# A two-layer hybrid attention block on one core: weights stored so that a partition's part of each load is one contiguous run

## The chip, the cores and the metric

The kernel runs on one core of one Trainium2 chip. The metric is the device time of one execution in microseconds (us), as the median of several runs; lower is better.

## The reference

Two layers of a diffusion trunk work on 512 latent tokens and 256 context tokens, 1024 wide, in float32. In each layer

```python
sh, sc, gt = split(silu(c) @ w_ada[l] + b_ada[l], 3)           # w_ada: 1024 x 3072, also for c_ctx
h  = rms_norm(x, norm_g[l]) * (1 + sc) + sh                    # latent and context rows
qa, ka, va, ga, qb, kb, vb, gb, qn, kn, vn, gn = split(h @ w_in[l])   # w_in: 1024 x 3584
ya = rms_norm(diff_attend(qa, ka, va)) * silu(ga)              # group A
yb = gqa_attend(qb, kb, vb) * silu(gb)                         # group B
yn = neighbourhood_attend(qn, kn, vn, rpb) * silu(gn)          # group C
x  = x + gt * (concat(ya, yb, yn) @ w_out[l])                  # w_out: 1024 x 1024
```

Latent queries attend to latent and context keys; context queries, in the first layer only, to context keys. Queries and keys are normalised, and those of A and B rotated. Only the latent rows of the second layer are returned.

## The kernel before

All activations are held transposed, 128 features on the partitions in KT = 8 blocks, 768 tokens on the free axis (512 latent, 256 context). The three large weights are the only big reads: 25 MB of `w_ada`, 29 MB of `w_in` and 8 MB of `w_out` for both layers, counted from their shapes.

**Modulation.** `w_ada` is read in blocks of 128 output columns, each as two DMAs of 256 KB (4 blocks of 128 input rows by 128 columns). For the first layer's shift and scale, 16 blocks are loaded in eight pairs by `ada_load` (issued at L185) into buffers that later hold probabilities (`hl`, `pt`) or spare ones (`adw`, `stg`), and `ada_pair` (matmuls at L198) turns each pair into a column of the scale and shift. `build_h` (L426 and after) needs that column for the block `kt` of normalised activations. The other 32 blocks come from the generator `ada_blocks` (L214), which is stepped now and then while projections run: its load (L221) goes into two `adw` buffers, one block ahead, its matmuls are at L236, and VectorE copies and adds at L241 to L250.

**Projections.** `w_in`'s columns are cut into ten chunks of 384 or 256 columns, listed in the dictionary `CH` by column ranges; chunk a1 is put together from two ranges (128 and 256 columns). Each chunk is loaded in four pieces of 256 input rows (two blocks of 128 partitions). `w_out` is loaded in four column blocks of 256 columns, in pieces of 2 or 3 input blocks (`OKT`). All these pieces go through one stream, `WStream`: `_load` (DMA at L69) into three `raw` buffers, then `_split`, which makes of each float32 weight a rounded part `whi` on ScalarE (L82) and a remainder `wlo` on VectorE or GpSimd (L85), with room for HLB = 6 split pieces. A piece that also needs the norm of value columns gets squares on ScalarE (L278). `done` frees a split piece and lets the stream advance. The projection matmuls (`mm3`, L685 to L687) multiply hi by hi, hi by lo and lo by hi; the output's are at L1093 to L1095.

**Attention.** For each unit of queries: scores on TensorE into two score tiles (L781), row maxima on VectorE (L836), exponentials on ScalarE (L850), a cast to float16 (L870) with a remainder on VectorE or GpSimd (L871), a transposing DMA `pt<-hl` (L873), and the product with the values (L906, L907). While a group's attention runs, `both` (L1060) mixes in the next chunks' projections.

**Order.** Every DMA is issued by SyncE (SP) in one order, and each engine works through its own list in order. The lists are fixed at build time: the program is written in Python in the order described, with priorities shifted for some steps (`prio`), and the tile framework then orders the instructions with a planner that runs a simulated timeline (L1355, `schedule_with_timeline_sim=True`). Its estimates of durations, those of DMAs included, can move instructions relative to each other.

The work begins with 3 MB of activations (L1205), then the eight pairs of modulation blocks, between them the first four pieces of `w_in` (chunk a0), whose projection `proj_first` interleaves with `ada_pair` and `build_h`.

Of the kernel before, what the change touches and what calls it, by code (L numbers as in the profile page):

```python
# [24 lines left out]
DEPTH = 2  # L25
D = 1024
KT = 8
# [5 lines left out]
BT = 6 * 256 + 6 * 192 + 256  # L33


REST = {"C": 7}
AK = [[6, 2, 0, 2], [0, 1, 0, 2]]
VSHARE = {"HA": (0, 1), "H": (0, 1), "G": (1, 1), "T": (1, 4), "HC": (1, 8), "WB": (1, 2), "WC": (1, 1),
# [71 lines left out]
def tile_hybrid_block(ctx: ExitStack, tc: tile.TileContext, xT_d, cT_d, ng_d, w_ada, bT_d, w_in, w_out,  # L110
# [7 lines left out]
    V, A, G, PE, SP = nc.vector, nc.scalar, nc.gpsimd, nc.tensor, nc.sync  # L118
# [56 lines left out]
    def ada_load(l, bs, spare=False):  # L175

        ts = []
        for b in bs:
            for r in range(2):
                if spare:  # L180
                    t = sb([128, 576], F32, "stg", 2) if r else sb([128, 512], F32, "adw", 2)
                else:
                    t = sb([128, 768], F32, *(("pt", 4) if r else ("hl", 4)))
                t = t[:, 0:512].rearrange("p (k n) -> p k n", n=128)
                SP.dma_start(out=t, in_=w_ada[l, 512 * r:512 * r + 512, 128 * b:128 * b + 128].rearrange(  # L185
                    "(k p) n -> p k n", p=128))
                ts.append(t)
        return l, bs, ts

# [24 lines left out]
    def ada_blocks(blocks):  # L214


        def load(l, b):
            ts = []
            for r in range(2):
                t = sb([128, 512], F32, "adw", 2).rearrange("p (k n) -> p k n", n=128)  # L220
                SP.dma_start(out=t, in_=w_ada[l, 512 * r:512 * r + 512, 128 * b:128 * b + 128].rearrange(  # L221
                    "(k p) n -> p k n", p=128))
                ts.append(t)
            return ts

        nxt = load(*blocks[0])
        yield
        for i, (l, b) in enumerate(blocks):
            if l not in mods:
                new_mods(l)  # L230
            ts = nxt
            ps = (psV if share.phase == "1" else psP).tile([128, 512], F32, tag="pv" if share.phase == "1" else "p",
                                                           name="ada")
            for r in range(2):
                for g in range(4):
                    PE.matmul(ps[32 * g:32 * g + 32, 0:128], lhsT=cS[:, 4 * r + g, :], rhs=ts[r][:, g, :],  # L236
                              start=(r == 0), stop=(r == 1), tile_position=(0, 32 * g))
            if i + 1 < len(blocks):
                nxt = prio(-100)(load)(*blocks[i + 1])
            t = sb([128, 128], F32, "adt", 1)  # L240
            V.tensor_copy(t, ps[:, 0:128])  # L241
            src = ps[:, 128:130]
            PE.matmul(src, lhsT=t, rhs=sel, start=True, stop=True)
            w, kt = divmod(b, 8)
            if w == 1:
                V.tensor_scalar(out=mods[l][0][:, kt, :], in0=src, scalar1=bT1[:, l, kt:kt + 1],
                                scalar2=ng[:, l, kt:kt + 1], op0=ALU.add, op1=ALU.mult)
            else:
                V.tensor_scalar(out=mods[l][1 if w == 0 else 2][:, kt, :], in0=src, scalar1=bT[:, l, b:b + 1],
                                scalar2=None, op0=ALU.add)  # L250
            yield

    def ada_step():
# [1 line left out]
        next(st["ada"], None)  # L255


    CH = {
# [4 lines left out]
    }  # L263
    FA = ["b0", "b1", "gb"]
    FB = ["c0", "c1", "c2", "gn"]
    FC = ["y", "o"]
# [1 line left out]
    F1 = ["a1", "ga"]  # L268
    ORDER = [c for c in ["a0"] + F1 + FA + FB + FC if c in CH]
    VCOL = {"a0": (256, 384), "a1": (0, 128), "b0": (128, 256), "c1": (0, 384)}  # L270
    vn = {}

    def v_norm(l, c, q):
        def emit(raw, lo):
            a, b = VCOL[c]
            if q == 0:
                vn[l, c] = sb([128, 8], F32, "vn" + c, 1)
            A.activation(out=lo[:, :, a:b], in_=raw[:, :, a:b], func=AF.Square,  # L278
                         accum_out=vn[l, c][:, q:q + 1])
        return emit  # L280

    OKT = {"ab": [(0, 3), (3, 2)], "n": [(5, 3)]}
    pieces, pidx = [], {}
    for l in range(DEPTH):
        for c in ORDER:
            cols, n = CH[c]
            pidx[l, c] = []
            for q in range(4):
                srcs, off = [], 0
                for c0, w in cols:  # L290
                    srcs.append((w_in[l, 256 * q:256 * q + 256, c0:c0 + w].rearrange("(k p) n -> p k n", p=128),
                                 off, w))
                    off += w
                pidx[l, c].append(len(pieces))
                pieces.append(("w", n, 2, srcs) + ((v_norm(l, c, q),) if c in VCOL else ()))
        for part in ("ab", "n"):
            for oc in range(4):
                pidx[l, part, oc] = []
                for k0, nk in OKT[part]:
                    src = w_out[l, 128 * k0:128 * k0 + 128 * nk, 256 * oc:256 * oc + 256].rearrange(  # L300
                        "(k p) n -> p k n", p=128)
                    pidx[l, part, oc].append(len(pieces))
                    pieces.append(("w", 256, nk, [(src, 0, 256)]))
    W = WStream(nc, pool, pieces, share)
# [348 lines left out]
    def ctx_cols(l, c):  # L653
        n = CH[c][1]
        if l == 0:
# [33 lines left out]
    def proj_first(l, c, groups, before):  # L689

        open_group(l, c[0].upper())
        n = CH[c][1]
        for gi, js in enumerate(groups):
# [366 lines left out]
    def both(l, g, chunks, lead=0):  # L1060
# [13 lines left out]
        for x, _ in enumerate(attn(l, g)):  # L1074
            want = min(nf, lead + (nf - lead - REST.get(g, 0)) * (x + 1) // (na - (YE if g == "B" else 0)))
            while done[0] < want:
# [213 lines left out]
def _layout(x, c, ctx, c_ctx, norm_g, w_ada, b_ada, w_in, w_out, diff_q_norm, diff_k_norm, lambda_q1, lambda_k1,  # L1290
            lambda_q2, lambda_k2, diff_subln, gqa_q_norm, gqa_k_norm, nat_q_norm, nat_k_norm, nat_rpb):
    import numpy as np

    ca = np.ascontiguousarray
    lat = np.asarray(x)[0].reshape(8, 64, D).transpose(1, 0, 2).reshape(NL, D)
    both = np.concatenate([lat, np.asarray(ctx)[0]], 0)
    d = {}
    d["xT"] = ca(both.T.reshape(KT, 128, NT).transpose(1, 0, 2))
    cc = np.stack([np.asarray(c)[0], np.asarray(c_ctx)], 1)
    d["cT"] = ca(cc.reshape(KT, 128, 2).transpose(1, 0, 2))  # L1300
    d["ng"] = ca(np.asarray(norm_g).reshape(DEPTH, KT, 128).transpose(2, 0, 1))
    d["w_ada"] = ca(np.asarray(w_ada))
    d["bT"] = ca(np.asarray(b_ada).reshape(DEPTH, 24, 128).transpose(2, 0, 1))
    d["w_in"] = ca(np.asarray(w_in))
    d["w_out"] = ca(np.asarray(w_out))
    d["small"] = ca(np.concatenate([np.asarray(a) for a in (
        diff_q_norm, diff_k_norm, gqa_q_norm, gqa_k_norm, nat_q_norm, nat_k_norm,
        lambda_q1, lambda_k1, lambda_q2, lambda_k2, diff_subln)], 1))
    f = np.float32
    t = np.arange(NL)  # L1310
    row, col = (t % 8).astype(f), (t // 8).astype(f)
    parts = []
    for dim in (32, 64):
        nf = dim // 4
        inv = np.power(f(10000.0), -np.arange(nf, dtype=f) / f(nf)).astype(f)
        ang = np.concatenate([row[:, None] * inv, col[:, None] * inv], 1).astype(f)
        parts += [np.cos(ang).astype(f), np.sin(ang).astype(f)]
    d["rope"] = ca(np.concatenate(parts, 1).reshape(4, 128, 96).transpose(1, 0, 2))
    rpb = np.asarray(nat_rpb)
    p = np.arange(128)  # L1320
    qi, qr = p // 8, p % 8
    k = np.arange(256)
    kw, kr = k // 8, k % 8
    tab = np.full((DEPTH, 128, BT), 0.0, f)
    ok = (kw[None] >= qi[:, None]) & (kw[None] < qi[:, None] + 16)
    dr = kr[None] - qr[:, None] + 7
    dc = np.clip(kw[None] - qi[:, None] + 7, 0, 30)
    qc = np.where(qi < 8, 56 + qi, qi - 8)
    kc = np.where((qi < 8)[:, None], 48 + kw[None, :128], kw[None, :128])
    dc3 = kc - qc[:, None] + 15  # L1330
    for h in range(6):
        g = rpb[:, h][:, dr, dc]
        g[:, ~ok] = -1e18
        tab[:, :, 256 * h:256 * h + 256] = g
        tab[:, :, 1536 + 192 * h:1536 + 192 * h + 128] = rpb[:, h][:, dr[:, :128], dc3]
    d["btab"] = tab
    return d
# [24 lines left out]
```

## Time and profile before

| | |
|---|---|
| three runs | 935.75, 937.06, 941.35 us; median 937.06 |
| profiled execution, device time | 930.04 us |
| its span in the trace | 928.2 us |
| mean granted TensorE clock | 0.95 |
| read from HBM, written to HBM | 86.55 MB, 15.47 MB |
| DMA packets | 361,449 |
| of these under 512 B | 256,656 |
| 512 B to under 2 KB | 98,560 |
| 2 KB to under 8 KB | 5,888 |

In the profile, PE is TensorE's matrix multiply and PEld its weight load, DVE is VectorE, ACT ScalarE, POOL GpSimd, SPq the queue of SyncE, which issues DMAs. A group of instructions is named by its line and as `out<-in` by tile names, so `raw<-in_w_in_dram` is a load of a projection piece and `pt<-hl` a transposing DMA. In a row of waits stand the engine and line that waited, the work that ended the wait, then the total in us, the number of times and the longest. In a row of one line or tile, three numbers with slashes are the shortest, median and longest duration in ns (in us where the row says so). The slices are fortieths of the span, a digit being tenths. In a row `q1 hardware_dynamic` stand packets, MB and the time that the packets took as a share of 16 DMA engines over the span or the stretch asked for; it can pass 100% where packets of one engine overlap.

### The profile page before, as it was taken

The page shows a single profiled execution, that of the slowest core. Times are in us where ns is not written, and L with a number is a line of the kernel's source. Part 1 is how long each engine was busy: PE and PEld are TensorE (multiplying, and loading weights), DVE is VectorE, ACT ScalarE, POOL GpSimd, SP SyncE. Part 2 cuts the span into 40 slices and gives each one's busy share as a digit, 9 for nine tenths or more (in the row PEclk, how much of TensorE's full clock was granted, in tenths as well). Part 3 has the DMA queues.
Part 4 walks back from the last instruction along what each step waited for, and adds up shares of the span by engine and source line. Part 5 has one row for each costly group of instructions (what it writes and reads, how often), then busy time and mean ns, then how long its engine had stood idle before and what let it go on. Part 6 is the DMA issues. An engine that isn't in the chain of part 4 may idle for free.

```text
span 928.2 us, 17966 instructions
## 1 busy us (share of the span) xinstructions
PE 829.5 (89%) x6386; PEld 709.7 (76%) x6386; DVE 682.7 (74%) x1306; ACT 592.3 (64%) x1269; POOL 541.3 (58%) x502
## 2 busy tenths in 40 slices
PE   5899997997998999797999989989959999988978
PEld 3788886786887889685777889878849888866757
DVE  5975788988678866467765797789877975855853
ACT  5334577885887687476563445478758978757740
POOL 2638846998798465432441047939988776732420
PEclk9899999998999999899999999999979999987979
DMA  9925895644979997989898713884556889995642
GB/s 307 331 90 135 204 215 133 154 85 127 194 156 221 195 221 170 227 213 229 183 234 235 243 61 101 184 189 101 140 132 156 168 188 249 240 253 134 134 114 83
DMA packets 361449, 165.47 MB, mean 178 GB/s; under 512 B 256656, under 2 KB 355216, under 8 KB 361104
## 3 DMA queue, kind: packets, MB, share of 16 engines
q1 hardware_dynamic: 361360, 164.33, 73.9%
q8 instruction: 50, 0.82, 0.4%
q14 instruction: 39, 0.32, 0.1%
HBM read 86.55 MB, written 15.47 MB: 110 GB/s over the span
## 4 chain that ended last, share of the span: by engine, by line
PE 46%; DVE 15%; DMA 13%; POOL 9%; issue 8%; ACT 7%; SPq 1%; DVEq 0%; POOLq 0%; ACTq 0%
PE proj L685 7%; PE proj L687 7%; PE proj L686 6%; PE sc L781 5%; DMA pt<-hl 4%; PE pv L906 3%; PE op L1093 3%; PE op L1094 3%; PE op L1095 2%; ACT p L850 2%; DVE mx L836 2%; DMA raw<-in_w_in_dram 2%; DMA stB<-in_btab_dram 2%; POOL hl L871 2%; POOL wlo L85 1%
## 5 line engine op out<-in xcount | busy, mean ns | idle before, releaser
L871 POOL TENSOR_TENSOR hl<-p,hl 128x768 f16<-128x768 f32 (+3 forms) x138 | 204.2, 1484 | 179.7 <-ACT hl L870 139.7
L685 PE MATMUL proj<-whi,bigL 128*128 128x384 f32 (+1 forms) x592 | 203.4, 344 | 9.8 <-DVE tb L608 3.8
L686 PE MATMUL proj<-wlo,bigL 128*128 128x384 f32 (+1 forms) x592 | 200.3, 338 | 0.9 <-POOL wlo L85 0.7
L687 PE MATMUL proj<-whi,bigL 128*128 128x384 f32 (+1 forms) x592 | 197.7, 336 | 0.0
L850 ACT ACTIVATE p<-sc,nb,gsc 128x768 f32<-128x768 f32 (+3 forms) x200 | 166.0, 844 | 14.3 <-DVE p L866 5.0
L836 DVE TENSOR_REDUCE mx<-sc 128x1 f32<-128x768 f32 (+2 forms) x128 | 118.7, 931 | 31.7 <-PE sc L781 31.2
L685 PEld LDWEIGHTS proj<-whi,bigL 128*128 128x128 f32 x592 | 115.4, 195 | 19.9 <-DVE tb L608 5.4
L870 ACT CAST hl<-p 128x768 f16<-128x768 f32 (+3 forms) x144 | 103.7, 725 | 33.0 <-DMA pt<-hl 18.5
L686 PEld LDWEIGHTS proj<-wlo,bigL 128*128 128x128 f32 x592 | 115.5, 195 | 3.9 <-POOL wlo L85 1.6
L687 PEld LDWEIGHTS proj<-whi,bigL 128*128 128x128 f32 x592 | 114.4, 194 | 3.3 <-issue 2.4
L85 POOL TENSOR_TENSOR wlo<-raw,whi 128x768 fp32r<-128x768 f32 (+1 forms) x44 | 82.9, 1893 | 30.0 <-ACT whi L82 24.8
L82 ACT CAST whi<-raw 128x768 fp32r<-128x768 f32 (+1 forms) x104 | 80.3, 779 | 30.8 <-DMA raw<-in_w_in_dram 16.2
L906 PEld LDWEIGHTS <-pt 128*128 128x128 f16 x736 | 65.9, 99 | 41.2 <-DMA pt<-hl 25.7
L85 DVE TENSOR_TENSOR wlo<-raw,whi 128x768 fp32r<-128x768 f32 (+1 forms) x60 | 65.2, 1090 | 25.3 <-ACT whi L82 22.5
L685 PE MATMUL proj<-whi,bigC 128*128 128x384 f32 (+2 forms) x224 | 75.8, 339 | 0.8 <-ACT xn L468 0.8
L686 PE MATMUL proj<-wlo,bigC 128*128 128x384 f32 (+2 forms) x224 | 74.8, 334 | 0.0
L687 PE MATMUL proj<-whi,bigC 128*128 128x384 f32 (+2 forms) x224 | 74.6, 335 | 0.0
L156 POOL TENSOR_TENSOR rsqb<-rsqb,half 128x12 f32<-128x12 f32 (+2 forms) x25 | 68.2, 2726 | 10.5 <-DVE rsqb L155 8.4
L907 PEld LDWEIGHTS <-pt 128*128 128x128 f16 x736 | 66.6, 100 | 4.2 <-issue 1.2
L906 PE MATMUL pv<-vA,pt 128*128 128x128 f16 (+2 forms) x424 | 52.2, 229 | 13.6 <-DMA pt<-hl 13.0
L838 ACT ACTIVATE nb<-mx,lnp,gsc 128x1 f32<-128x1 f32 (+1 forms) x104 | 39.6, 385 | 37.6 <-DVE mx L836 26.5
L781 PE MATMUL sc<-bigL 128*128 128x512 f16 (+4 forms) x184 | 46.1, 310 | 17.3 <-ACT p L850 16.7
(320 smaller groups left out, 2042.2 us busy)
## 6 DMA issues: line engine op xcount, KB each, us to landing
raw<-in_w_in_dram SPq DMA_DIRECT2D x56, 384.0 KB, 4.1
adw<-in_w_ada_dram SPq DMA_DIRECT2D x68, 256.0 KB, 3.8
raw<-in_w_in_dram SPq DMA_DIRECT2D x24, 256.0 KB, 3.6
raw<-in_w_out_dram SPq DMA_DIRECT2D x16, 384.0 KB, 4.0
g_d<-tb SPq DMA_DIRECT2D x20, 192.0 KB, 2.6
gt<-g_d SPq DMA_DIRECT2D x18, 192.0 KB, 2.9
hl<-in_w_ada_dram SPq DMA_DIRECT2D x12, 256.0 KB, 5.0
pt<-in_w_ada_dram SPq DMA_DIRECT2D x12, 256.0 KB, 5.2
```

Of the source, the lines that this page charges most:

```text
L82: self.nc.scalar.copy(out=hi, in_=raw2)
L85: self.share("W").tensor_tensor(out=lo, in0=raw2, in1=hi.bitcast(F32), op=ALU.subtract)
L156: G.tensor_tensor(out=y, in0=x, in1=half[:, 0:n], op=ALU.pow)
L685: PE.matmul(ps, lhsT=xh, rhs=hi, start=(kt == 0), stop=False)
L686: PE.matmul(ps, lhsT=xh, rhs=lo, start=False, stop=False)
L687: PE.matmul(ps, lhsT=xl, rhs=hi, start=False, stop=(kt == KT - 1))
L781: PE.matmul(ps, lhsT=q, rhs=k, start=n == 0, stop=n == b[2] - 1)
L836: V.tensor_reduce(out=mx[:, 0:ns], in_=ps[:, 0:w * ns].rearrange("p (a b) -> p a b", b=w), axis=AX.X, op=ALU.max)
L850: A.activation(out=p[:, w * x:w * x + w], in_=u["ps", i][:, w * x:w * x + w], func=AF.Exp, bias=u["nb", i][:, x:x + 1], scale=lc[l]["sc"][ ...
L870: A.copy(out=hl[:, 0:n], in_=p)
L871: lo_eng.tensor_tensor(out=hl[:, n:2 * n], in0=p, in1=hl[:, 0:n], op=ALU.subtract)
L906: PE.matmul(po[r, :], lhsT=pt[:, b, r], rhs=V_[:, vt, c0:129], start=first, stop=False)
```

## The change

The three weights are stored in another order in DRAM, and the loads are written for that order. The host prepares the arrays; that is outside the device time. No instruction of a compute engine is changed, nor the number of bytes or their places in SBUF.

- `w_ada` becomes [layer, block of 128 columns, 128 partitions, 8 input blocks, 128 columns]. A load of four input blocks is 2048 contiguous bytes of each partition, where it was four runs of 512 bytes.
- `w_in` becomes [layer, piece of 256 input rows, 128 partitions, 2 x 3584], with the chunks one after the other in the order of their names and in each chunk both input blocks of a partition together: 3072 or 2048 contiguous bytes, where it was two runs of 1536 or 1024. Chunk a1, whose two ranges were loaded by two DMAs a piece (128 KB and 256 KB), is stored joined and loaded by one.
- `w_out` becomes [layer, column block, 128 partitions, 8 input blocks, 256 columns]: 3072 or 2048 contiguous bytes, where it was three or two runs of 1024.
- `CH` moves to the module's top, since the host code uses it as well.

```diff
@@ ada_load, and the same in ada_blocks' load
-                SP.dma_start(out=t, in_=w_ada[l, 512 * r:512 * r + 512, 128 * b:128 * b + 128].rearrange(
-                    "(k p) n -> p k n", p=128))
+                SP.dma_start(out=t, in_=w_ada[l, b, :, 4 * r:4 * r + 4, :])
@@ the list of pieces
         for c in ORDER:
-            cols, n = CH[c]
+            n, c0 = CH[c][1], sum(v[1] for k, v in CH.items() if k < c)
             pidx[l, c] = []
             for q in range(4):
-                srcs, off = [], 0
-                for c0, w in cols:
-                    srcs.append((w_in[l, 256 * q:256 * q + 256, c0:c0 + w].rearrange("(k p) n -> p k n", p=128),
-                                 off, w))
-                    off += w
+                src = w_in[l, q, :, 2 * c0:2 * c0 + 2 * n].rearrange("p (k n) -> p k n", n=n)
                 pidx[l, c].append(len(pieces))
-                pieces.append(("w", n, 2, srcs) + ((v_norm(l, c, q),) if c in VCOL else ()))
+                pieces.append(("w", n, 2, [(src, 0, n)]) + ((v_norm(l, c, q),) if c in VCOL else ()))
...
-                    src = w_out[l, 128 * k0:128 * k0 + 128 * nk, 256 * oc:256 * oc + 256].rearrange(
-                        "(k p) n -> p k n", p=128)
+                    src = w_out[l, oc, :, k0:k0 + nk, :]
@@ _layout, on the host
-    d["w_ada"] = ca(np.asarray(w_ada))
+    d["w_ada"] = ca(np.asarray(w_ada).reshape(DEPTH, KT, 128, 24, 128).transpose(0, 3, 2, 1, 4))
...
-    d["w_in"] = ca(np.asarray(w_in))
-    d["w_out"] = ca(np.asarray(w_out))
+    w = np.asarray(w_in).reshape(DEPTH, 4, 2, 128, -1)
+    d["w_in"] = ca(np.concatenate([
+        np.concatenate([w[..., a:a + n] for a, n in CH[c][0]], 4).transpose(0, 1, 3, 2, 4).reshape(DEPTH, 4, 128, -1)
+        for c in sorted(CH)], 3))
+    d["w_out"] = ca(np.asarray(w_out).reshape(DEPTH, KT, 128, 4, 256).transpose(0, 3, 2, 1, 4))
```

More of the change, by code (lines that the diff above doesn't have):

```diff
@@ L33 @@
 BT = 6 * 256 + 6 * 192 + 256
+CH = {
[4 rows of a table added]
+}
 REST = {"C": 7}
@@ L220, in load @@
                 t = sb([128, 512], F32, "adw", 2).rearrange("p (k n) -> p k n", n=128)
-                SP.dma_start(out=t, in_=w_ada[l, 512 * r:512 * r + 512, 128 * b:128 * b + 128].rearrange(
-                    "(k p) n -> p k n", p=128))
+                SP.dma_start(out=t, in_=w_ada[l, b, :, 4 * r:4 * r + 4, :])
                 ts.append(t)
@@ L255, in ada_step @@
         next(st["ada"], None)
-    CH = {
[4 rows of a table removed]
-    }
     FA = ["b0", "b1", "gb"]
```

8 rows, old and new, of the table CH are left out of this document.

## The prediction, made before the change was run

> **What bounds the kernel now.** I read the page first: busy shares, the slices, the queue, the chain and the issues.
>
> ```profile
> span 928.2 us, 17966 instructions
> PE 829.5 (89%) x6386; PEld 709.7 (76%) x6386; DVE 682.7 (74%) x1306; ACT 592.3 (64%) x1269; POOL 541.3 (58%) x502
> ...
> DMA  9925895644979997989898713884556889995642
> ...
> q1 hardware_dynamic: 361360, 164.33, 73.9%
> ...
> PE 46%; DVE 15%; DMA 13%; POOL 9%; issue 8%; ACT 7%; SPq 1%; DVEq 0%; POOLq 0%; ACTq 0%
> PE proj L685 7%; PE proj L687 7%; PE proj L686 6%; PE sc L781 5%; DMA pt<-hl 4%; PE pv L906 3%; PE op L1093 3%; PE op L1094 3%; PE op L1095 2%; ACT p L850 2%; DVE mx L836 2%; DMA raw<-in_w_in_dram 2%; DMA stB<-in_btab_dram 2%; POOL hl L871 2%; POOL wlo L85 1%
> ...
> raw<-in_w_in_dram SPq DMA_DIRECT2D x56, 384.0 KB, 4.1
> adw<-in_w_ada_dram SPq DMA_DIRECT2D x68, 256.0 KB, 3.8
> ```
>
> PE is busy for 89% of the span, so at most 11% is open to anything that is not matmul work. The DMA engines are busy 73.9% of the time, 686 us each, and stand at 9 in many slices. Yet only 13% of the chain is DMA, and its largest piece, 4%, is the transposes of the probabilities (pt<-hl), which the change doesn't touch. So the question is how much of the weights' transfer time comes through to PE. The stages, from the table by windows:
>
> ```profile
> 23.00:46.00 23.00, 20.43 (x187) 17.20 (x183) 22.32 (x66) 8.02 (x20) 14.29 (x19) 0.85 1.10 331
> 46.00:70.00 24.00, 21.72 (x192) 18.82 (x190) 18.68 (x51) 8.65 (x22) 7.76 (x6) 1.00 0.32 96
> ...
> 250.00:360.00 110.00, 103.80 (x846) 89.22 (x845) 83.55 (x156) 85.91 (x164) 77.46 (x62) 0.97 0.86 189
> 360.00:530.00 170.00, 154.35 (x1214) 129.10 (x1213) 108.15 (x237) 97.70 (x204) 53.26 (x50) 0.96 0.88 225
> ```
>
> The columns are the length, the busy time of PE, PEld, DVE, ACT and POOL, the clock, the DMA share and GB/s. From 23 to 46 us the DMA engines are full (1.10), but so is DVE: 22.32 of 23 us. From 250 to 530 DMA stands at 0.86 and 0.88 while PE is busy 258 of 280 us. Last the waits, of which these touch the change:
>
> ```profile
> PE pv L906 <- DMA pt<-hl: 18.8, 19, 3.1
> ACT whi L82 <- DMA raw<-in_w_in_dram: 16.2, 10, 3.6
> ACT whi L82 <- DMA raw<-in_w_out_dram: 5.2, 4, 2.3
> PE ada L236 <- DMA adw<-in_w_ada_dram: 4.8, 6, 2.0
> PE ada L198 <- DMA adw<-in_w_ada_dram: 1.0, 1, 1.0
> ```
>
> PE itself stands for modulation weights for 5.8 us in all, never for the projections' (ACT does, for 21.4 us, ahead of its casts), and 18.8 us for transposes.
>
> **The change part by part.** *Packet lengths.* It leaves the bytes and every engine instruction as they are. Modulation: 96 DMAs of 256 KB go from 4 runs of 512 B per partition to one of 2048 B. Projections: 64 pieces go from 2 runs of 1536 B (a1: 2 each of 512 and 1024) to one of 3072 B, 16 from 2 of 1024 to one of 2048. Output: 16 pieces go from 3 of 1024 to one of 3072 B, 8 from 2 of 1024 to 2048. That a run becomes one packet although the access is written in two dimensions is seen where 4 DMAs read [128, 2, 512] contiguously (x_d, the second row below). Four stretches in which nearly all data packets have one length give the cost of each length, from the DMA view; the rows of x_d first:
>
> ```profile
> L1139 SPq DMA_DIRECT2D x_d<-bigL x8: 319/338/339, 518.6 to 534.4; - x8
> L1105 SPq DMA_DIRECT2D bigC<-x_d x4: 339/403/477, 771.9 to 786.7; - x4
> ```
> ```profile
> DMA packets 1334, 0.70 MB, mean 352 GB/s; under 512 B 41, under 2 KB 1334, under 8 KB 1334
> ...
> q1 hardware_dynamic: 1334, 0.70, 115.1%
> ```
> ```profile
> DMA packets 507, 0.73 MB, mean 365 GB/s; under 512 B 32, under 2 KB 507, under 8 KB 507
> ...
> q1 hardware_dynamic: 507, 0.73, 97.4%
> ```
> ```profile
> DMA packets 369, 0.66 MB, mean 330 GB/s; under 512 B 47, under 2 KB 47, under 8 KB 369
> ...
> q1 hardware_dynamic: 369, 0.66, 86.5%
> ```
> ```profile
> DMA packets 367, 0.92 MB, mean 306 GB/s; under 512 B 151, under 2 KB 151, under 8 KB 367
> ...
> q1 hardware_dynamic: 367, 0.92, 93.8%
> ...
> pt<-hl SPq DMA_TRANSPOSE x2, 8.5
> ```
>
> They are 17 to 19 us (512 B, modulation), 217.5 to 219.5 (1536 B), 520.5 to 522.5 (2048 B, the store of x_d) and 775.5 to 778.5 (the load of x_d; 216 packets over 2 KB make up nearly all of 0.92 MB, so 4 KB each). Share times 16 engines times length over the data packets: 36.8/1334 = 27.6 ns (the small ones counted in), 31.2/475 = 65.6, 27.7/322 = 86, 45/216 = 208 at most. In bytes per ns: 18.6, 23.4, 23.8, 19.7. So 512 B is slow, and beyond 1536 B nothing shows a gain.
>
> *Modulation transfers.* 4 x 27.6 = 110.4 ns become 86, 24.4 less; a DMA has 8 such runs on each engine: 0.195 us. Over 96: 18.7 us of each engine's 686, or 2.7%. With x_d's 19.7 B/ns, 104 ns, it would be 0.05 us, 4.9 in all.
>
> The Trainium skill, DMA: Bandwidth & Descriptors, section Specifications, puts line rate at transfers of 512 B and more. By it these runs are at line rate already and this term is zero; the rows above disagree, with 18.6 against 23.8 B/ns.
>
> *Projections and output.* No packet of 3072 B is in this trace. From 2048's rate it takes 129 ns, from x_d's 156; before, 131. For 80 pieces of 8 runs an engine: from -1.3 to +16 us of engine time. The 2048 B ones are equal, or 3.3 us worse at x_d's rate. I take zero, as its length lies between both rows and the second was measured on one tensor alone.
>
> *What of it reaches PE.* Before 46 us, 32 modulation loads save 32 x 0.195 = 6.2 us, but DVE is the cover there with 0.7 us to spare, and PE's only wait for them is L198's 1.0 us: I take -0.5 (0 to -0.8, four loads' saving). If DVE were faster, the 6.2 us would count. Later blocks load one ahead in two adw buffers; PE's 6 waits at L236 last 0.8 us on average, and a block's two loads are issued one behind the other, so 2 x 0.195 x 6 = -2.3 (0 to -4.8, all of them). For ACT's 14 waits at L82: zero, as the length's price is (+2.8 at most, 14 x 0.2; -0.2).
>
> *Transposes.* These share the 16 engines, and so wait behind fewer busy nanoseconds.
>
> ```profile
> DMA to landing us min/median/max: 2.2/3.6/10.2
> ```
>
> By this row for pt, with the shortest taken as unhindered, 1.4 of 3.6 us is time behind others. pt<-hl holds 4% of the chain, 37 us, so some 14.4 us is queueing, an estimate. A load 2.7% smaller takes 0.4 us off if queueing goes with load; if it goes with busy over idle share, 0.88 going to 0.856 takes 19%, 2.7 us, and 0.739 to 0.719 takes 10%. I take the middle of these two, 14%: -2.0. What is late next is the cast and subtraction ahead of the transposes, which nothing here hastens.
>
> *SP.* The 8 second parts of a1 fall away. SP issues all these DMAs in one order:
>
> ```profile
> L69 SPq DMA_DIRECT2D raw<-in_w_in_dram x88: 363/419/1502, 12.1 to 785.6; - x88
> ```
>
> 8 x 0.419 = 3.4 us less on SP, spread over eight places; SP's share of the chain is 1%, so zero (0 to -3.4).
>
> Sum: -0.5 - 2.3 - 2.0 = -4.8 us. The profiled execution took 930.04 us, 1.8 more than its span; the runs' median is 937.06 (935.75 to 941.35), 0.8% above it. So 925 for a profiled run and **932** as a median, with a range of its own from 925 (all ends that gain: -12) to 939.5 (+2.4, the raw waits' loss less the surest queueing). A measurement of this kernel can tell about 1% from no change, 9.4 us.
>
> **The rivals.** *DMA sets the pace where it is full.* If the order on PE and DVE merely follows the data in the first 46 us and from 250 to 530, the engine time saved there returns whole.
>
> ```profile
> adw<-in_w_ada_dram SPq DMA_DIRECT2D x24, 256.0 KB, 4.1
> ```
>
> 24 such loads lie between 250 and 530 us, 32 ahead of 46: 56 x 0.195 = 10.9, and the L236 waits, all outside these stretches, 2.3: 13.2 us, **924**. For it: shares of 0.86 to 1.10. Against it: PE's 258 of 280 us and DVE's 22.32 of 23. If all 18.7 us came back it would be 918.
>
> *The order turns against the softmax.* The kernel's instructions are put in order at build time by a planner with DMA times of its own, and L69 issues 8 DMAs fewer. Where weights come sooner in that plan, their casts on ACT (L82) can move ahead of exponentials (L850) in ACT's fixed order, and PE's next scores wait for a free score bank.
>
> ```profile
> PE sc L781 <- ACT p L850: 18.9, 16, 3.9
> ...
> L82 ACT CAST whi<-raw 128x768 fp32r<-128x768 f32 (+1 forms) x104 | 80.3, 779 | 30.8 <-DMA raw<-in_w_in_dram 16.2 <-DMA raw<-in_w_out_dram 5.2 <-PE proj L687 4.1
> ```
>
> A cast is 0.779 us. If 16 more of the 104 came to stand in the way, as many as there are such waits today, it is +12.5 us: **949.5**. From 13 on it is over 1%. For it: that wait is there already. Against it: six split buffers (HLB) keep casts from running far ahead, and waits for the projections' weights are few, so their places need not move.
>
> *Longer packets are no faster, or none come about.* At x_d's rate throughout, modulation gains 4.9 us and the rest loses 16 + 3.3: +14.4 us of engine time. That is 2.1% more load; the queueing of 14.4 us grows by 9 to 20% (0.739 to 0.755, 0.88 to 0.898, busy over idle), some 2 us: **939**, within 1%. Were the runs sent in pieces as before, it would be 937. For it: x_d's 306 GB/s against 352 for 512 B. Against it: x_d's load shares its stretch with transposes, and the store's 86 ns are at 2048 B.
>
> x_d's partitions lie 16 KiB apart, and the new modulation's and output's 4 and 8 KiB, powers of two as well. The same page of the Trainium skill (section Latency and other measured facts) tells of copies losing up to half their rate at row pitches of large powers of two, measured from 512 KiB up; no run here has such a pitch, and the page gives no price for this one.
>
> **How the numbers follow.** The forecast 0.35, DMA's pace 0.28, the casts 0.22, no faster packets 0.15. Faster by over 1% (below 927.7): 0.28, and 0.02 from the forecast's lower edge: 0.30. Slower by over 1% (above 946.4): 0.22. Within: 0.48. The range goes from 918, all engine time returned, to 950, the casts' price; more of either is left out.
>
> **What would show it.** In the changed profile: some 54,000 packets fewer (49,152 to 12,288 for modulation, the rest for the other two) at the same bytes; the DMA share down from 73.9% by about 2 points; the first 46 us no shorter by more than 1 us, with DVE as full; waits at L236 about half; pt<-hl landing in 3.4 to 3.5 us (3.6 less 14% of 1.4); L82's waits as they were. Wrong it would be if the stages from 250 to 530 shrank by 4 us or more (DMA's pace), if sc <- p waits doubled (the casts), or if the DMA share stood still (no faster packets).

## The result, and the profile after

The changed kernel took 924.31 us (median of four runs, 922.72 to 926.84), the kernel before 939.2 us beside it (935.75 to 941.9): ratio 0.987, 95% interval 0.9837 to 0.9902. (The two medians alone give 0.984, inside this interval.) Two later comparisons gave 0.9871 (0.9845 to 0.9897) and 0.9869 (0.9841 to 0.9897). So it is faster by 1.3%, some 12 us, where 932 against 937 (0.5%) was forecast. Two executions of the unchanged kernel in the later comparisons took 1948 and 2526 us; they count in none of the ratios.

The page of the changed kernel:

```profile
span 922.5 us, 17964 instructions
PE 825.3 (89%) x6386; PEld 706.9 (77%) x6386; DVE 679.0 (74%) x1306; ACT 592.4 (64%) x1269; POOL 541.3 (59%) x502
...
DMA  9834895645979996998898713784557899996642
...
DMA packets 307049, 165.46 MB, mean 179 GB/s; under 512 B 256528, under 2 KB 275216, under 8 KB 306704
...
q1 hardware_dynamic: 306960, 164.33, 73.7%
...
raw<-in_w_in_dram SPq DMA_DIRECT2D x64, 384.0 KB, 4.0
adw<-in_w_ada_dram SPq DMA_DIRECT2D x68, 256.0 KB, 3.6
```

There are 54,400 packets fewer, as foreseen, and the runs did become single packets. But the DMA share stands at 73.7% after 73.9%, and the engines' busy times are those of before within 5 us. The span is 5.7 us shorter than in the profile before, half of what the runs show: that first profile caught one of the kernel's fastest executions (930.04 us, below each of its four runs). A second profile of the same kernel has a span of 937.6 us. Differences of a few us between two single profiles therefore say little here, and below I compare many.

Line numbers are those of the changed kernel from here on: L69 became L76, L82 L89, L236 L241, L685 to L687 L679 to L681, L781 L775, L850 L844, L906 L900 and L1093 to L1095 L1087 to L1089. The waits that the prediction watched, after the change:

```profile
PE pv L900 <- DMA pt<-hl: 14.9, 14, 3.0
ACT whi L89 <- DMA raw<-in_w_in_dram: 14.0, 10, 3.2
PE ada L241 <- DMA adw<-in_w_ada_dram: 5.2, 7, 2.1
PE sc L775 <- ACT p L844: 19.7, 17, 3.9
```

In this pair the wait for transposes is 3.9 us shorter (18.8 before), L241's no smaller than L236's 4.8 us, and the scores' wait for exponentials as it was (18.9). For L241 one pair says too little: over the six profiles whose later modulation blocks have short runs it is 4.8 to 8.0 us (mean 6.6), over the eight with long ones 3.8 to 5.2 (mean 4.6). The stretch that DMA filled before, by windows:

```profile
23.00:46.00 23.00, 19.84 (x184) 16.42 (x185) 21.41 (x63) 7.28 (x18) 14.46 (x19) 0.85 0.88 306
```

The DMA share fell from 1.10 to 0.88, and PE did no more than before (19.84 us busy, 20.43 before), while DVE is busy for 21.41 of 23 us. So the transfers became shorter where the prediction said, and the 12 us are not there: the stage up to group A's first score takes 108.6 us on average in the old order of instructions and 108.0 in the new (table below).

One thing that no view of one profile shows: which part of the change altered the instruction lists. No compute instruction was changed, but their order was. Contiguous runs alone leave the order as it was: in the traces of such kernels the instructions of TensorE, VectorE, ScalarE and GpSimd come in the order of the kernel before, line by line. Loading a1 by one DMA instead of two makes the planner order the engines anew. In the traces ScalarE's instructions differ first at 41 us, VectorE's at 48 us; TensorE's matmuls differ at nine places near 59 us and then from the 2755th on (393 us), just ahead of group C in the first layer. At 1687 of 6386 places a matmul of another line stands. That splits the change into two parts that can be run one without the other.

### The profile page after: what moved, and what is told of

Read it like the earlier page. It is cut to its first block, busy times and chain, and to the rows that moved or that the text cites. A ratio compares the mean times of both kernels' runs of the same rounds, so it can differ in the third digit from the quotient of the medians.

```text
span 922.5 us, 17964 instructions
## 1 busy us (share of the span) xinstructions
PE 825.3 (89%) x6386; PEld 706.9 (77%) x6386; DVE 679.0 (74%) x1306; ACT 592.4 (64%) x1269; POOL 541.3 (59%) x502
## 3 DMA queue, kind: packets, MB, share of 16 engines
q1 hardware_dynamic: 306960, 164.33, 73.7%
## 5 line engine op out<-in xcount | busy, mean ns | idle before, releaser
L679 PE MATMUL proj<-whi,bigL 128*128 128x384 f32 (+1 forms) x592 | 203.0, 344 | 8.4 <-DVE tb L602 4.2
L681 PE MATMUL proj<-whi,bigL 128*128 128x384 f32 (+1 forms) x592 | 197.3, 335 | 0.0
L844 ACT ACTIVATE p<-sc,nb,gsc 128x768 f32<-128x768 f32 (+3 forms) x200 | 166.4, 846 | 10.6 <-DVE p L860 4.7
L679 PEld LDWEIGHTS proj<-whi,bigL 128*128 128x128 f32 x592 | 115.2, 195 | 18.7 <-DVE tb L602 5.9
L681 PEld LDWEIGHTS proj<-whi,bigL 128*128 128x128 f32 x592 | 114.6, 194 | 2.8 <-issue 2.0
L89 ACT CAST whi<-raw 128x768 fp32r<-128x768 f32 (+1 forms) x104 | 80.3, 780 | 28.4 <-DMA raw<-in_w_in_dram 14.0
L900 PEld LDWEIGHTS <-pt 128*128 128x128 f16 x736 | 65.5, 99 | 35.3 <-DMA pt<-hl 20.9
L679 PE MATMUL proj<-whi,bigC 128*128 128x384 f32 (+2 forms) x224 | 76.0, 339 | 1.0 <-ACT xn L462 1.0
L681 PE MATMUL proj<-whi,bigC 128*128 128x384 f32 (+2 forms) x224 | 74.1, 333 | 0.0
L901 PEld LDWEIGHTS <-pt 128*128 128x128 f16 x736 | 66.0, 100 | 4.3 <-issue 2.2
L775 PE MATMUL sc<-bigL 128*128 128x512 f16 (+4 forms) x184 | 46.4, 312 | 18.0 <-ACT p L844 17.2
L900 PE MATMUL pv<-vA,pt 128*128 128x128 f16 (+2 forms) x424 | 51.3, 228 | 9.6 <-DMA pt<-hl 9.2
```

The lines of the kernel that those rows point to most:

```text
L89: self.nc.scalar.copy(out=hi, in_=raw2)
L679: PE.matmul(ps, lhsT=xh, rhs=hi, start=(kt == 0), stop=False)
L681: PE.matmul(ps, lhsT=xl, rhs=hi, start=False, stop=(kt == KT - 1))
L844: A.activation(out=p[:, w * x:w * x + w], in_=u["ps", i][:, w * x:w * x + w], func=AF.Exp, bias=u["nb", i][:, x:x + 1], scale=lc[l]["sc"][ ...
L900: PE.matmul(po[r, :], lhsT=pt[:, b, r], rhs=V_[:, vt, c0:129], start=first, stop=False)
L901: PE.matmul(po[r, 0:65 - c0], lhsT=pt[:, nb + b, r], rhs=V_[:, vt, c0:65], start=False, stop=stop)
```

## The experiments

Theory after the result: the gain comes from the order that the planner makes when a1 is one DMA. Rivals: longer packets (the change's own purpose), and the eight DMAs that SP no longer issues.

**Only a1 joined**, short runs kept; the compute engines' instructions come in the order of the changed kernel (the code in this section is shortened):

```diff
-for c0, w in cols: srcs.append((w_in[l, 256 * q:256 * q + 256, c0:c0 + w].rearrange(...), off, w))
+src = w_in[l, 256 * q:256 * q + 256, c0:c0 + n].rearrange("(k p) n -> p k n", p=128)   # chunks' columns stored side by side
```

> Only a1's two column ranges are stored side by side, so that its piece is one DMA instead of two: 8 DMAs fewer, and the instruction lists of all engines are those of the changed kernel; all runs keep their old lengths (512, 1024, 1536 B). If the gain comes from longer packets: ratio to before 0.998 to 1.003. If it comes from the DMAs saved on SP and the order that the planner makes of the rest: 0.985 to 0.990. If DMA share and order each do part: 0.993.

Measured: 0.9917 (0.9886 to 0.9948), 927.55 against 935.9 us. Two thirds of the gain without one longer packet, but for a1's rows, whose pieces of 512 and 1024 B are joined to 1536 B.

Its page also explains why the DMA share of the changed kernel hardly fell:

```profile
q1 hardware_dynamic: 359184, 164.33, 75.4%
```

The new order alone has a share of 75.4%, of a shorter span: 698 us of engine time, against 686 and 692 in two profiles of the kernel before. Against this run the changed kernel's 73.7% is 1.7 points lower, near the 2 foreseen.

**Long runs everywhere, a1 by two DMAs**; the compute engines' instructions come in the order of the kernel before:

```diff
-pieces.append(("w", n, 2, [(src, 0, n)]) + ...
+pieces.append(("w", n, 2, [(src[:, :, 0:128], 0, 128), (src[:, :, 128:384], 128, 256)] if c == "a1" else [(src, 0, n)]) + ...
```

> The changed layout for all three weights, but a1's pieces are loaded by two DMAs each as before (runs of 512 and 1024 B), so that the lists of all engines are those of the kernel before. Longer packets: 0.987 to 0.990. Order and fewer DMAs: 0.998 to 1.003.

Measured: 0.9969 (0.9942 to 0.9995). Long packets are worth 0.3% in the old order. In the new one it is 0.9871/0.9917 = 0.995.

**Only the modulation weights contiguous**, all else as before:

> Only the modulation weights get their contiguous runs (512 to 2048 B); order and the rest as before. Longer packets: nearly the whole gain, 0.988 to 0.991, since my rows gave the other weights none. Order: 0.998 to 1.003. My own forecast of its reach would be 0.995.

Measured: 0.9942 (0.9917 to 0.9967), what I had forecast for the whole change (0.995), and nothing like the 0.988 to 0.991 of the packets' theory. From here to all three weights it goes from 0.9942 to 0.9969: runs of 3072 B on projections and output added nothing that can be seen (the intervals overlap).

**The changed kernel on the same chip:**

> The changed kernel itself on the same chip as the three others: 0.984 to 0.990 by every theory. It gives the size that the parts have to add up to, and a second profile.

Measured: 0.9871. The parts add up: 0.9917 x 0.9942 = 0.986.

**The kernel before, again**, for a second profile:

> The kernel before itself, with its text moved to the lines of the changed one. 0.998 to 1.002 by every theory; it gives a second profile of before, whose first was one of its fastest executions, and the noise of a comparison.

Measured: 0.9979 (0.9948 to 1.0009), no difference, with the profiled execution at 937.6 us of span.

**Eight DMAs put back elsewhere.** a1 joined, but ga's pieces by two DMAs of 128 columns, all runs short. SP issues as many as before. In the traces the instructions of the four compute engines come line by line in the order of the joined kernel; only SP's list is another.

```diff
+pieces.append(("w", n, 2, [(src[:, :, 0:128], 0, 128), (src[:, :, 128:n], 128, n - 128)] if c == "ga" else [(src, 0, n)]) + ...
```

> As the run that only joined a1, but ga's pieces of 256 columns are loaded as two DMAs of 128 columns each: 8 DMAs more again, so as many as before, with short runs; TensorE's list is that of the joined kernel but for a few places. If the gain of the joining lies in the 8 DMAs that SP doesn't issue: 0.998 to 1.003. If it lies in TensorE's new order: 0.989 to 0.995.

Measured: 0.9881 (0.9835 to 0.9927). The DMAs that SP is spared are not the cause: with all of them back the gain is still there, and so are as many packets as before (361,449).

**Both parts without long projections and outputs:**

> The two parts that gained alone, together: contiguous modulation weights and a1 joined; projections and output keep their old runs. If the parts add up: 0.986 (0.9917 x 0.9942), and not slower than the whole change; if runs of 3072 B cost something, 0.002 to 0.003 faster than the whole change. If 3072 B runs gain: 0.988 to 0.990.

Measured: 0.9864 (0.9827 to 0.99). The change's whole gain comes from these two parts; whether 3072 B runs cost 0.1% or nothing can't be told.

**A third order.** The same, with c2's pieces split as a1's were:

```diff
-... if c == "ga" else [(src, 0, n)]) + ...
+... if c == "c2" else [(src, 0, n)]) + ...
```

> a1 joined, c2's pieces of 384 columns split in two DMAs instead (128 and 256 columns, just what a1's were): number and sizes of DMAs as before, all runs short, and a third order on all engines. DMA count: 0.998 to 1.003. Order: anything from 0.985 to 1.010, going with the time that TensorE's clock stands at half (94 to 108 us in the profiles with the old order, 85 to 91 with the new).

Measured: 0.998 (0.9951 to 1.0009). It issues as many DMAs as the kernel before and as the run with ga split (0.9881). An order can thus also bring nothing; it isn't the joining as such that gains, nor a1's longer rows, which this run has too. Nor did the time go with the clock as expected: over its twelve executions the mean granted clock was 0.955, above the 0.952 to 0.954 of the changed kernel in its three comparisons, and the time was that of before.

**Where the modulation's part lies.** Contiguous runs for the first 16 blocks only, and for the 32 later ones only, both in the old order:

```diff
-in_=w_ada[l, 512 * r:512 * r + 512, 128 * b:128 * b + 128].rearrange("(k p) n -> p k n", p=128)
+in_=w_ada[l, b, :, 4 * r:4 * r + 4, :]      # in outline: in ada_load only, or in ada_blocks' load only; both layouts stored
```

> In the old order, only the 16 modulation blocks ahead of 46 us get contiguous runs of 2048 B; the 32 later ones keep 512 B runs (both layouts are stored). If the modulation's gain (0.994) is that of the DMA-full start: 0.994. By my forecast, DVE covers it: 0.999 to 1.000.

> The counterpart: only the 32 later blocks get contiguous runs. By my forecast nearly the whole gain of the modulation's layout is here: 0.994 to 0.996 (4.3 of 4.8 us). If the gain is in the start: 0.999 to 1.000.

Measured: 0.9986 (0.9962 to 1.001) and 0.9974 (0.9947 to 1.0002). Neither is clear of no change. The first interval leaves out 0.994, so the start alone doesn't hold the whole gain; beyond that the middle values go with the forecast's division, the start covered and the rest counting, but don't prove it. Together they make 0.996.

**A version to beat both**, contiguous modulation, a1 joined, ga split:

> The parts that gained alone, together: contiguous modulation weights, a1 joined and ga's pieces in two DMAs (0.9881 without the modulation's part); projections and output keep short runs. If the modulation's 0.994 adds to it: 0.982 to 0.984, faster than the changed kernel by 0.3 to 0.5%. If the split of ga only scattered by chance: 0.986.

> The changed kernel once more on the chip of the last three, for the comparison with the best version: 0.984 to 0.990.

Measured: 0.9916 (0.9894 to 0.9938), slower than the changed kernel beside it (0.9869). The 0.994 of the modulation did not add to the 0.9881 of this order. A miss. The compute engines' order is the same in both, and long runs did what they do to the transfers (a DMA share of 72.9%, after 75.0% with short ones). The clock differs: over its six executions the mean granted clock was 0.949, against 0.953 with short runs and 0.954 in the changed kernel beside it. Why it was lower, or whether the 0.9881 was at the good end of its interval, stays open.

### Where the order gains

The marks of group A's, B's and C's first score matmul and of the last store of x_d cut each trace into seven stages. Six profiles have the old order (with short and long runs), seven the new (the run with ga split counted in). Means, with the range:

| stage, us | old order | new order |
|---|---|---|
| start to A, layer 1 | 108.6 (107.5 to 110.3) | 108.0 (106.7 to 110.2) |
| A to B | 152.1 (150.6 to 153.4) | 152.5 (151.7 to 153.4) |
| B to C | 133.1 (130.7 to 134.2) | 133.6 (130.8 to 135.8) |
| C to the end of the layer's output | 143.5 (140.3 to 146.2) | 136.9 (135.3 to 139.3) |
| to B, layer 2 | 190.5 (189.4 to 193.1) | 191.3 (190.3 to 192.5) |
| B to C | 92.6 (92.2 to 93.6) | 85.5 (84.6 to 85.8) |
| C to the end | 111.4 (110.1 to 112.2) | 115.4 (114.7 to 116.9) |

Three stages differ with no overlap of the ranges, whatever the layout: -6.6, -7.1 and +4.0 us. The rest differs by less than 1 us each; the spans differ by 8.7 us (931.8 and 923.1 in the mean). The windows of the last stages and of the first layer's B and C, of the kernel before (second profile):

```profile
262.90:396.30 133.40, 121.22 (x1001) 105.88 (x1000) 93.50 (x172) 94.90 (x163) 83.71 (x61) 0.95 0.89 198
396.30:542.30 146.00, 136.74 (x999) 110.72 (x999) 95.23 (x215) 80.85 (x171) 38.90 (x42) 0.93 0.85 216
...
733.00:826.60 93.60, 88.45 (x706) 76.96 (x704) 69.65 (x101) 75.14 (x125) 67.60 (x45) 1.00 0.98 209
826.60:937.60 111.00, 94.78 (x676) 74.68 (x674) 62.74 (x132) 56.55 (x112) 29.39 (x25) 0.88 0.56 146
```

and with only a1 joined:

```profile
259.50:393.70 134.20, 123.11 (x1034) 107.50 (x1033) 94.72 (x178) 95.20 (x164) 84.31 (x61) 0.96 0.92 199
393.70:533.00 139.30, 128.53 (x969) 103.16 (x968) 92.93 (x209) 80.34 (x170) 37.90 (x42) 0.95 0.90 223
...
725.10:810.90 85.80, 81.76 (x665) 70.58 (x665) 62.20 (x93) 72.20 (x121) 63.30 (x42) 1.00 1.00 212
810.90:925.80 114.90, 96.70 (x716) 77.29 (x712) 66.49 (x137) 57.15 (x114) 31.03 (x27) 0.92 0.63 152
```

The counts in brackets show what moved. In the first layer some 30 PE instructions (by their lines, 20 projection matmuls, L679 to L681, and 10 products with values, L900 and L901) now stand ahead of group C's first score instead of behind it. The B stage takes them in with no loss of time (133.4, 134.2), and the C stage is rid of them. In the second layer it is the other way round: some 40, most of them projections, leave B for the last stage. B gains 7.8 us between these two profiles, the last stage loses 3.9.

It looks as if they filled gaps on PE, but the rows say otherwise. The length of a stage less PE's busy time is what PE waits: in the first layer's B and C stages 12.2 and 9.3 us in the old order, 11.1 and 10.8 in the new; in the second layer's B and last stage 5.2 and 16.2, then 4.0 and 18.2. Over the whole span PE waits 99 us in the old order and 98 in the new (means of the six and the seven profiles). What shrinks is its busy time: 832.9 us become 824.7, for the same 6386 matmuls. These 8.2 us are nearly all of the 8.7. The profiles with short runs alone, two of each order, say the same: spans of 932.9 and 925.5 us, busy times of 832.7 and 824.6.

The clock goes with it. The traces record when TensorE ran at half speed; PE's work inside these pieces sums to 80 us in the old order (72 to 86) and 64 in the new (54 to 71). A matmul takes about twice as long there (last section), so 16 us less of it should save 8 us, an estimate that meets the 8.2. Over all 14 profiles, every us of work at half speed goes with 0.49 us more of busy time (correlation 0.99). So by the record the new order's gain is matmul work that no longer runs at half speed, and not filled gaps. Why less of it does is not shown: neither the moved instructions nor the clock was changed alone.

The third order (0.998) has the first layer's gain, and loses it in the second:

```profile
397.90:532.90 135.00, 126.30 (x964) 101.92 (x963) 91.92 (x209) 79.57 (x170) 39.21 (x42) 0.96 0.90 229
532.90:729.00 196.10, 169.85 (x1215) 153.58 (x1216) 156.03 (x271) 124.03 (x293) 147.29 (x141) 0.92 0.56 128
729.00:818.40 89.40, 83.82 (x659) 71.92 (x658) 69.95 (x93) 72.00 (x122) 62.45 (x42) 1.00 0.90 200
818.40:934.90 116.50, 99.70 (x731) 80.69 (x730) 67.41 (x142) 58.74 (x118) 35.04 (x28) 0.91 0.59 152
```

135 us as the new order, but 196.1 us for the stage with group A (190.5 in the old order), 89.4 and 116.5 for the last two (92.6 and 111.4). Here PE waits 103.6 us in all, more than in any other profile: an order can also lose by its waits, whatever the clock.

## Why the prediction was right or wrong

The direction was right and the time of 924 us lay in the range; the mechanism of the forecast gave 5 us, and 12 came. That 924 lay in the range is partly luck: its lower end, 918, was set by a rival whose mechanism did not act, and most of the gain came from an order for which the sum has no term.

*The step that failed* is that on SP: "The 8 second parts of a1 fall away ... so zero (0 to -3.4)". As a saving on SP zero was right, as the run with eight DMAs put back shows. But fewer DMAs also mean another order, and that was worth 0.83% (0.9917), 7.8 us, more than all terms of the sum. I had the order among the rivals with one sign only: casts ahead of exponentials, 949.5. The scores' waits didn't double (18.9 to 19.7 us), and the order moved projection matmuls between stages instead, with 16 us less of PE's work at half speed. Nothing in the profile before told which way the planner would move them, or that the clock would follow.

*Modulation, on PE:* forecast -4.8 us for the sum, of which this layout bore all; measured 0.9942, 5.4 us of 935.9. Right in size, and by the two partial runs in place as far as they can tell. Of the terms only the wait for the later blocks can be seen: L241's mean of 6.6 us with short runs became 4.6 with long ones, -1.9 from the unrounded values where -2.3 was forecast (4.4 in the run with this part alone, after 4.8 and 7.1). The other 3 us or so of the 5.4 are not accounted for.

*Modulation, on the DMA engines:* the term was 18.7 us of engine time. In the old order, with this part alone, the share was 73.2% of 930.8 us, 681 us, against 686 and 692 in the two profiles of before: 5 to 11 us. In the new order it is the forecast's size: joined alone 698 us, with long modulation runs 678; with ga split 694, then 675: 20 and 19 us. So the term is not shown to be wrong, and two profiles of one kernel already differ by 6 us. With few other packets beside them, the price of 2048 B was right too:

```profile
DMA packets 445, 0.81 MB, mean 407 GB/s; under 512 B 48, under 2 KB 48, under 8 KB 445
...
q1 hardware_dynamic: 445, 0.81, 105.6%
```

From 595 to 597 us of the changed kernel, 397 packets of 2048 B: 33.8/397 = 85 ns, 86 foreseen. In the mean of a whole kernel packets stay longer: 29 to 30 ns for 512 B in the two profiles of before, and some 100 ns for the 2048 B ones that replace them with this part alone, which makes the term 13 to 16 us.

*Projections and output:* zero was right in time (0.9864 without their long runs, 0.9871 with), for a reason that I had wrong in part. I took 129 to 156 ns for a packet of 3072 B:

```profile
DMA packets 297, 0.81 MB, mean 407 GB/s; under 512 B 32, under 2 KB 32, under 8 KB 297
...
q1 hardware_dynamic: 297, 0.81, 101.3%
```

From 218 to 220 us, 265 of them took 32.4 us, 122 ns or 25.1 bytes per ns, faster than my best bound. In the mean of the whole kernel, though, such a packet takes 169 ns, slower than my worst, and one of 1536 B 79 to 81 ns: two short ones took some 160. So in company of other packets these weights had nothing to gain on the engines. The 156 ns came from x_d's load, which had transposes beside it.

*No faster packets* (rival, 939 us). Its sign, a share that stands still, came true between the two pages (73.9 and 73.7%), and yet the rival was wrong: 2048 B did go faster, and the new order raised the share by about as much as the long runs lowered it. This sign didn't tell the two apart either.

*Transposes:* -2.0 us forecast, from pt<-hl landing in 3.4 to 3.5 us. It lands in 3.7 us with the modulation's part alone and 3.8 in the changed kernel (3.6 before, 3.9 with only a1 joined); the term did not show.

*DMA's pace* (rival, 924 us). Its number came true, and so did its sign: the stages from B to the first layer's end shrank by 6 us. But they shrink as much with short runs and a1 joined, and not with long runs in the old order (144.1 us for the stage from C on). A right number for a wrong reason: the sign I had named did not tell this rival from a change of order.

## What to carry to other kernels

Where a planner orders the instructions, a change in the number of DMAs can also draw a new order: compare the instruction lists first, and run the part that changes them apart from the part that doesn't. Give such a part a range of both signs; here it was -0.8% and -1.2% for two kernels with the same order on the compute engines (their intervals overlap) and -0.2% for a third order. When the same matmuls take less busy time, look at the granted clock before looking for filled gaps. Longer DMA runs pay by the stage that waits for them: in the old order 512 to 2048 B was worth 0.6% (0.3 to 0.8), 1536 to 3072 B nothing that could be measured.

## What the runs showed of the hardware

The granted clock goes with the order, though not strictly. In the means of the runs it was 0.946 to 0.948 for the kernel before and 0.952 to 0.954 for the changed one; but 0.949 in one kernel of the new order, and 0.955 in the third order, which gained nothing. The clock record of the traces counts 95 to 108 us at half speed in the six profiles of the old order and 75 to 95 in the seven of the new, in pieces of 3.4 us and multiples. One such piece in the kernel before (second profile), in the second layer's last stage, lasts from 841.8 to 855.5 us, four times 3.4. The 3.4 us ahead of it and the piece itself, by windows, and some of PE's rows:

```profile
838.40:841.80 3.40, 1.18 (x7) 0.75 (x8) 2.43 (x5) 1.71 (x5) 1.27 (x1) 1.00 0.93 302
841.80:855.50 13.70, 11.07 (x28) 7.83 (x29) 6.85 (x15) 9.34 (x17) 2.17 (x2) 0.50 0.46 168
```
```profile
839.95 0.66 PE L640 MATMUL yt<-ident,xn 128*128 128x128 f32 x4 [2.53 <-DVE tb L602]
...
854.31 0.63 PE L1088 MATMUL op<-bigL,whi 128*128 128x512 f32 x1
854.74 0.63 PE L1089 MATMUL op<-bigL,wlo 128*128 128x512 f32 x1
855.17 0.53 PE L1087 MATMUL op<-bigL,whi 128*128 128x512 f32 x1
855.54 0.39 PE L1088 MATMUL op<-bigL,whi 128*128 128x512 f32 x1
855.77 0.40 PE L1089 MATMUL op<-bigL,wlo 128*128 128x512 f32 x1
```

Up to 855 us a matmul takes 0.63 us and starts 0.43 us after the one before, then 0.39 and 0.23. The Trainium skill, TensorE: Matmul & The Clock Gate, Part 1, says that the clock drops to half after an idle window of about 3.4 us and needs as long a busy one to come back; the pieces' length agrees. The idle window does not: ahead of this drop PE waited 2.53 us at a stretch and was busy for 1.18 of 3.40 us, so here less than a wholly idle window was enough.

PE's busy time sums to 829 to 836 us in the six profiles of the old order and to 820 to 828 in the seven of the new, for the same count of matmuls; the work at half speed accounts for it (above). Whether the clock is the cause or follows the order's waits was not tried.

The unchanged kernel's runs spread over 930 to 946 us, wider than most parts measured here, so that only many runs side by side on one chip could tell them apart.
